# Summing the modulation over partitions: 32x32 transposes and small copies in place of products with ones

## The chip, the core and the metric

The kernel runs on one core of a Trainium2 chip. The core has five engines with a queue each that is worked in order: TensorE (PE, with its weight loads shown as PEld), VectorE (DVE), ScalarE (ACT), GpSimd (POOL) and SyncE (SP), which here issues nearly all transfers. The metric is the device time of one execution in microseconds (us); lower is better. A profile is one further execution, recorded by the hardware.

## The reference, cut to what matters

Two decoder layers of width 1024 over 512 tokens, each an attention (stick-breaking in layer 0, forgetting in layer 1) and a gated MLP of width 2816. Every layer is steered by a vector `mod` of 6 x 1024 numbers, which is made from the conditioning vector `c`:

```python
c_act = jax.nn.silu(c)
for i in range(DEPTH):
    mod = jnp.einsum('bd,dm->bm', c_act, w_mod[i]) + b_mod[i]
    sh_a, sc_a, gt_a, sh_f, sc_f, gt_f = jnp.split(mod, N_MOD, axis=-1)
    h = modulate(rmsnorm(x, g_mix_pre[i]), sh_a, sc_a)          # h * (1 + scale) + shift
    ...                                                         # qkv, attention, w_o
    x = x + gt_a[:, None, :] * rmsnorm(o, g_mix_post[i])
    h = modulate(rmsnorm(x, g_ffn_pre[i]), sh_f, sc_f)
    ...                                                         # gate, up, conv, silu, down
    x = x + gt_f[:, None, :] * rmsnorm(y, g_ffn_post[i])
```

All is float32. `mod` is a product of one row of 1024 numbers with a 1024 x 6144 matrix per layer. Its six parts of 1024 numbers (SH_A, SC_A, GT_A, SH_F, SC_F, GT_F) are needed in two shapes: the shifts and scales as columns (channel d*128+p on partition p, a tile of 128 x 8), the gates as rows that are the same on all 128 partitions (128 x 1024).

## The kernel before, in words

TensorE does every large product as three products of float32r halves (`mm3`, L320 to L322: high times high, low times high, high times low). Weights come as tiles of 128 x 1024 by SP (`raw`, L252, tile `wf`, three buffers), ScalarE writes the rounded half `wh` (L246), VectorE or GpSimd the rest `wl` (L247). `ws.need` loads two tiles ahead of the one that TensorE is about to use. In the MLP's first stage one iteration `f` of 22 has 24 products for `gate` and 24 for `up` (tile `pgu`, 128 x 512 each), then `conv_act` (tiles `cv`, `yh`, `yl`) on ScalarE and VectorE, which there also makes both `wl`.

The parts of `mod` are made in the background of other stages, by generators that are stepped at fixed places:

- `mod_part` makes GT_F of layer 0 and five parts of layer 1 during the MLP of layer 0, and GT_F of layer 1 during the MLP of layer 1. After every iteration `f` from 2 on, `bg.step(4)` takes four steps. Eight steps load one 512 KB tile `wm` each (L142) and add it, times a column of silu(c), into `acc` (128 x 1024, L146, VectorE; the first addition of a column part is L144). So each partition p of `acc` holds the sum over d of the terms of row d*128+p, and what is left is the sum over the 128 partitions. For that `acc` is split into `ah` and `al` (L149, L151), and a product with a 128 x 128 matrix of ones puts the sum on all partitions (L163, L164: two products for each half of 512 columns, tile `pm`). A gate is then multiplied by its norm's weights `gp` (L166). A shift or scale is on every partition in full, and the wanted column of 128 is its diagonal, taken eight times with a product by the identity and a sum (`diagonal`, L131).
- `mod_part_pe` makes GT_A, SC_F and SH_F of layer 0 during layer 0's attention, with the sum over rows on TensorE (L202), four row groups apart, each in its own 32 partitions. For a shift or scale ScalarE copies the result to `mf` (L209), four 128 x 128 transposes on TensorE (L220) turn it, and VectorE adds the four groups (L221).
- `begin` makes SH_A and SC_A of layer 0; the change does not touch it.

The order on PE and SP is the order of the program text; the other three engines are ordered by a scheduler when the program is built, except in `begin`. Tiles `wm`, `ah`, `al`, `gp`, `gb` share three buffers of 128 x 1024 (`t4`), and SP waits at a load until its buffer is free, with all later loads behind it.

Of the kernel before, what the change touches and what calls it, by code (L numbers as in the profile page):

```python
# [8 lines left out]
F32 = mybir.dt.float32  # L9
F32R = mybir.dt.float32r  # L10
BF16 = mybir.dt.bfloat16
AF = mybir.ActivationFunctionType
ALU = mybir.AluOpType
AX = mybir.AxisListType

P = 128
# [21 lines left out]
def trunk(ctx, tc, x, c, w_mod, b_mod, g_mix_pre, g_mix_post, w_qkv, w_o, w_fg, b_fg,  # L38
# [8 lines left out]
    def nm(s):  # L47
        serial[0] += 1
        return f"{s}_{serial[0]}"

    def bank(s="b"):
        return pp.tile([P, 512], F32, tag="bank", name=nm(s), bufs=8)
# [7 lines left out]
    def t4(s, dt=F32):  # L60
        return sb.tile([P, D], dt, tag="t4", name=nm(s), bufs=3)
# [4 lines left out]
    def junk(n=512):  # L66
        return sb.tile([P, n], BF16, tag=f"junk{n}", name=nm("junk"), bufs=1)
# [58 lines left out]

    made = {}

    def diagonal(dst, src):

        nc.vector.tensor_tensor_reduce(junk(P), src, idn, 1.0, 0.0, op0=ALU.mult, op1=ALU.add, accum_out=dst)  # L131

    def mod_part(l, comp):
        row = comp in (GT_A, GT_F)
# [5 lines left out]
        for d in range(ND):  # L140
# [4 lines left out]
            else:  # L145
                nc.vector.scalar_tensor_tensor(acc, w, csil[:, d : d + 1], acc, op0=ALU.mult, op1=ALU.add)  # L146
            yield
        ah = t4("ah", F32R)
        nc.scalar.copy(ah, acc)  # L149
        al = t4("al", F32R)  # L150
        nc.vector.tensor_tensor(al, acc, ah.bitcast(F32), op=ALU.subtract)  # L151
        if row:
            res = sb.tile([P, D], F32, tag="gt", name=nm("gt"), bufs=2)
            gp = t4("gp")
            g = (g_mix_post if comp == GT_A else g_ffn_post)[l]
            nc.sync.dma_start(gp, g.rearrange("(o n) -> o n", o=1).to_broadcast([P, D]))
        else:
            res = cst.tile([P, ND], F32, name=nm("mc"))
        yield
        for h in range(2):  # L160
            cs = slice(512 * h, 512 * h + 512)
            ps = bank("pm")
            nc.tensor.matmul(ps, ones, ah[:, cs], start=True, stop=False)  # L163
            nc.tensor.matmul(ps, ones, al[:, cs], start=False, stop=True)  # L164
            if row:
                nc.vector.tensor_tensor(res[:, cs], ps, gp[:, cs], op=ALU.mult)  # L166
            else:
                for j in range(4):
                    diagonal(res[:, 4 * h + j : 4 * h + j + 1], ps[:, j * P : (j + 1) * P])
            yield  # L170
        if not row:
            nc.vector.tensor_tensor(res, res, b_col(l, comp), op=ALU.add)
            if comp in (SC_A, SC_F):
# [3 lines left out]
    def mod_part_pe(l, comp):  # L177
# [7 lines left out]
        for h in range(2):  # L185
# [18 lines left out]
            if row:  # L204
                a = slot("mh"), slot("ml")
                split(*a, ps)
            else:
                f = slot("mf", F32)
                nc.scalar.copy(f, ps)  # L209
            yield  # L210
            ps = bank("pm")
            cs = slice(512 * h, 512 * h + 512)
            if row:
                for i in range(2):
                    nc.tensor.matmul(ps, ones, a[i], start=i == 0, stop=i == 1)
                nc.vector.tensor_tensor(res[:, cs], ps, gb[:, 512:], op=ALU.add)
                nc.vector.tensor_tensor(res[:, cs], res[:, cs], gb[:, :512], op=ALU.mult)
            else:
                for j in range(4):
                    nc.tensor.transpose(ps[:, j * P : (j + 1) * P], f[:, j * P : (j + 1) * P], idn)  # L220
                nc.vector.tensor_reduce(res[:, 4 * h : 4 * h + 4], ps.rearrange("p (j q k) -> p j q k", q=4, k=32)[:, :, :, 0], axis=AX.X, op=ALU.add)  # L221
        if not row:
            nc.vector.tensor_tensor(res, res, b_col(l, comp), op=ALU.add)
            if comp in (SC_A, SC_F):
# [3 lines left out]
    class Background:  # L228
        def __init__(self, parts, make=mod_part):
            self.gens = [make(*p) for p in parts]  # L230

        def step(self, n=1):
            while n and self.gens:
                try:
                    next(self.gens[0])
                    n -= 1
                except StopIteration:
                    self.gens.pop(0)

# [747 lines left out]
```

## Time and profile before

| what | value |
|---|---|
| median of 3 runs | 1270.32 us (1270.16 to 1272.4) |
| the profiled execution's own time | 1270.56 us |
| its span, first to last instruction | 1268.8 us |
| mean granted TensorE clock | 0.999 |
| busy: PE, PEld | 1245.5 us (98%), 1029.5 us (81%) |
| busy: DVE, ACT, POOL | 680.4 us (54%), 597.9 us (47%), 268.4 us (21%) |
| layer 0: attention about, then MLP from | 65 to 240 us, 290 us |
| moved by DMA | 169.71 MB, 134 GB/s over the span |

The span is 1.8 us shorter than the execution's time, which also has what lies around the first and last instruction. Shares are means over all stages. Rows of a timeline give the start, the length and, in brackets, how long the engine had stood idle and whose work ended that. Matmuls are pipelined, so that a row of 0.39 us may start 0.23 us after the row above it.

### The profile page before, as it was taken

The numbers are of one execution on the slowest core, as the hardware profiler recorded it, in microseconds if no ns is written. First come the engines' busy times: TensorE is split into PE (matmuls) and PEld (weight loads), VectorE is DVE, ScalarE is ACT, GpSimd is POOL, SyncE is SP. The second block draws the span as 40 slices with busy tenths as digits, with TensorE's granted clock in tenths as the row PEclk, the third lists the DMA queues.
The fourth block names the chain that finished last, engine by engine and source line by source line (L and its number), as shares of the span: only waits on it lengthen the run. The fifth ranks groups of instructions, "written<-read, shape, count | busy, mean of one in ns | idle before, by whom it ended". The sixth has DMA issues, their size and how long they took to land.

```text
span 1268.8 us, 16979 instructions
## 1 busy us (share of the span) xinstructions
PE 1245.5 (98%) x6380; PEld 1029.5 (81%) x6380; DVE 680.4 (54%) x1157; ACT 597.9 (47%) x1117; POOL 268.4 (21%) x302
## 2 busy tenths in 40 slices
PE   6999999999999999999999999999999999999997
PEld 5877878789887888888887888877988888888886
DVE  6655444366788886422263565564685444442233
ACT  7577656565333334311375655664743333332121
POOL 4764544610000000000215554352000000000000
PEclk9999999999999999999999999999999999999999
DMA  9746424325587875223504344243073333332231
GB/s 296 213 147 219 126 92 159 89 78 165 167 248 223 275 223 160 86 98 100 151 1 129 123 133 116 90 128 104 26 248 95 94 99 100 100 100 87 96 100 67
DMA packets 178358, 169.71 MB, mean 134 GB/s; under 512 B 6984, under 2 KB 151776, under 8 KB 178275
## 3 DMA queue, kind: packets, MB, share of 16 engines
q1 hardware_dynamic: 178098, 168.56, 43.4%
q8 instruction: 50, 0.82, 0.3%
q14 instruction: 34, 0.27, 0.1%
q10 hardware_dynamic: 176, 0.07, 0.0%
HBM read 166.44 MB, written 2.16 MB: 133 GB/s over the span
## 4 chain that ended last, share of the span: by engine, by line
PE 84%; DVE 5%; ACT 4%; DMA 4%; issue 1%; POOL 1%; SPq 0%; ACTq 0%; POOLq 0%; DVEq 0%
PE pgu L321 11%; PE pgu L322 11%; PE pgu L320 11%; PE pd L321 6%; PE pd L320 6%; PE pd L322 6%; PE pqk L320 4%; PE pqk L322 4%; PE pqk L321 4%; PE ps L442 3%; PE po L492 3%; PE pv L320 3%; PE pv L322 3%; PE pv L321 3%; PE pa L480 2%; DMA wf<-in_w_ffn_gate_dram 2%
## 5 line engine op out<-in xcount | busy, mean ns | idle before, releaser
L246 ACT CAST wh<-wf 128x1024 fp32r<-128x1024 f32 (+2 forms) x178 | 185.3, 1041 | 313.0 <-PE pd L322 134.6
L321 PE MATMUL pgu<-htl,wh 128*128 128x512 f32 (+1 forms) x736 | 276.4, 376 | 0.6 <-DVE htl L382 0.6
L320 PE MATMUL pgu<-hth,wh 128*128 128x512 f32 (+1 forms) x736 | 276.4, 376 | 0.0
L322 PE MATMUL pgu<-hth,wl 128*128 128x512 f32 (+1 forms) x736 | 276.1, 375 | 0.0
L247 DVE TENSOR_TENSOR wl<-wf,wh 128x1024 fp32r<-128x1024 f32 x122 | 149.3, 1224 | 216.2 <-ACT wh L246 214.0
L321 PEld LDWEIGHTS pgu<-htl,wh 128*128 128x128 f32 x736 | 138.5, 188 | 26.2 <-DVE htl L382 1.0
L320 PEld LDWEIGHTS pgu<-hth,wh 128*128 128x128 f32 x736 | 138.5, 188 | 25.1
L322 PEld LDWEIGHTS pgu<-hth,wl 128*128 128x128 f32 x736 | 138.5, 188 | 24.8
L247 POOL TENSOR_TENSOR wl<-wf,wh 128x1024 fp32r<-128x1024 f32 (+3 forms) x56 | 129.7, 2320 | 122.6 <-ACT wh L246 110.4
L333 POOL TENSOR_TENSOR r<-v,mhalf 128x1 f32<-128x1 f32 x32 | 17.6, 549 | 449.1 <-DVE v L329 449.1
L320 PE MATMUL pd<-wh,yh 128*128 128x512 f32 x288 | 112.0, 389 | 0.0
L321 PE MATMUL pd<-wl,yh 128*128 128x512 f32 x288 | 112.0, 389 | 0.0
L322 PE MATMUL pd<-wh,yl 128*128 128x512 f32 x288 | 112.0, 389 | 0.0
L320 PE MATMUL pqk<-hth,wh 128*128 128x512 f32 (+1 forms) x240 | 94.3, 393 | 0.0
L322 PE MATMUL pqk<-hth,wl 128*128 128x512 f32 (+1 forms) x240 | 92.2, 384 | 0.3 <-POOL wl L247 0.3
L321 PE MATMUL pqk<-htl,wh 128*128 128x512 f32 (+1 forms) x240 | 92.1, 384 | 0.0
L899 ACT ACTIVATE cv<-cv 128x512 f32<-128x512 f32 x44 | 27.8, 632 | 108.8 <-DVE cv L898 102.6
L146 DVE SCALAR_TENSOR_TENSOR acc<-wm,csil,acc 128x1024 f32<-128x1024 f32 x52 | 66.7, 1283 | 14.0 <-DMA wm<-in_w_mod_dram 13.1
L320 PE MATMUL pv<-wh,hth 128*128 128x256 f32 (+1 forms) x224 | 68.6, 306 | 0.9 <-ACT hth L685 0.9
L322 PE MATMUL pv<-wh,htl 128*128 128x256 f32 (+1 forms) x224 | 66.9, 299 | 0.0
L321 PE MATMUL pv<-wl,hth 128*128 128x256 f32 (+1 forms) x224 | 66.7, 298 | 0.0
L320 PEld LDWEIGHTS pd<-wh,yh 128*128 128x128 f32 x288 | 54.1, 188 | 11.3
(208 smaller groups left out, 2209.7 us busy)
## 6 DMA issues: line engine op xcount, KB each, us to landing
wm<-in_w_mod_dram SPq DMA_DIRECT2D x80, 512.0 KB, 5.8
wf<-in_w_ffn_gate_dram SPq DMA_DIRECT2D x44, 512.0 KB, 4.9
wf<-in_w_ffn_up_dram SPq DMA_DIRECT2D x44, 512.0 KB, 4.8
wf<-in_w_ffn_down_dram SPq DMA_DIRECT2D x44, 512.0 KB, 3.5
wf<-in_w_qkv_dram SPq DMA_DIRECT2D x41, 512.0 KB, 5.6
wm<-in_w_mod_dram SPq DMA_DIRECT2D x32, 256.0 KB, 5.4
wf<-in_w_o_dram SPq DMA_DIRECT2D x16, 512.0 KB, 3.5
cum<-cumd SPq DMA_DIRECT2D x16, 512.0 KB, 5.6
```

What stands on the lines that cost most here:

```text
L146: nc.vector.scalar_tensor_tensor(acc, w, csil[:, d : d + 1], acc, op0=ALU.mult, op1=ALU.add)
L246: nc.scalar.copy(hi, src)
L247: (engine or nc.vector).tensor_tensor(lo, src, hi.bitcast(F32), op=ALU.subtract)
L320: nc.tensor.matmul(ps, ah, bh, start=first, stop=False)
L321: nc.tensor.matmul(ps, ah, bl, start=False, stop=False)
L322: nc.tensor.matmul(ps, al, bh, start=False, stop=last)
L333: nc.gpsimd.tensor_tensor(r, v, mhalf, op=ALU.pow)
L442: nc.tensor.matmul(ps[:, :n], q[hd][:, qs], k[hd][i][:, :n], start=i == 0, stop=i == 1)
L480: nc.tensor.transpose(ps[:, c : c + P], probs[qb][:, kb * P : (kb + 1) * P], idn)
L492: nc.tensor.matmul(po[HD * hd : HD * hd + HD, kb * P :], vt[p // 4, kb][:, e : e + HD], at[hd][kb], start=kb == 0, stop=kb == NT - 1, tile ...
L899: nc.scalar.activation(a, a, AF.Silu)
```

## The change

`mod_part` no longer splits `acc` and multiplies by ones. VectorE turns every 32 x 32 block of `acc` (`tr`) and adds along the free dimension (`part`, 128 x 32): now the 32 partitions of each quarter are summed, and four partial sums are left in four groups of 32 partitions. GpSimd copies the four groups side by side onto partitions 0 to 31 (`quad`), VectorE adds them (`qsum`). A column part is then put on its partitions by four small copies on GpSimd. A gate is turned once more (`gtr`, 32 x 32), written to DRAM as a row of 1024 numbers (`gtd`), read back to all 128 partitions (`gb`), and multiplied by `gp`. In `mod_part_pe` the same is done for shifts and scales from PSUM, with the small copies on VectorE. A step may now yield True, which ends a `bg.step(4)` early, so that a gate's write, read and multiplication fall into separate iterations.

```diff
+    def quadrants(src, n, engine):
+
+        u = sb.tile([32, P], F32, tag="quad", name=nm("quad"), bufs=1)[:, : 4 * n]
+        s = sb.tile([32, 32], F32, tag="qsum", name=nm("qsum"), bufs=1)[:, :n]
+        for i in range(4):
+            engine.tensor_copy(u[:, i * n : (i + 1) * n], src[32 * i : 32 * i + 32])
+        nc.vector.tensor_reduce(s, u.rearrange("p (i b) -> p b i", i=4), axis=AX.X, op=ALU.add)
+        return s
+
+    def columns_of(res, s, engine):
+
+        for j in range(4):
+            engine.tensor_copy(res[32 * j : 32 * j + 32, :], s.rearrange("p (d j) -> p j d", j=4)[:, j, :])
...
-        ah = t4("ah", F32R)
-        nc.scalar.copy(ah, acc)
-        al = t4("al", F32R)
-        nc.vector.tensor_tensor(al, acc, ah.bitcast(F32), op=ALU.subtract)
+        turned, part = t4("tr"), sb.tile([P, 32], F32, tag="part", name=nm("part"), bufs=1)
+        nc.vector.transpose(turned, acc)
+        nc.vector.tensor_reduce(part, turned.rearrange("p (b c) -> p b c", c=32), axis=AX.X, op=ALU.add)
         if row:
-            res = sb.tile([P, D], F32, tag="gt", name=nm("gt"), bufs=2)
             gp = t4("gp")
...
+        yield
+        s = quadrants(part, 32, nc.gpsimd)
+        if row:
+            rows = sb.tile([32, 32], F32, tag="gtr", name=nm("gtr"), bufs=1)
+            nc.vector.transpose(rows, s)
+            yield True
+            line = dr.tile([1, D], F32, name=nm("gtd"))
+            nc.sync.dma_start(line.rearrange("o (b r) -> (o b) r", r=32), rows)
+            yield True
+            wide = t4("gb")
+            nc.sync.dma_start(wide, line.to_broadcast([P, D]))
+            yield True
+            res = sb.tile([P, D], F32, tag="gt", name=nm("gt"), bufs=2)
+            nc.vector.tensor_tensor(res, wide, gp, op=ALU.mult)
         else:
             res = cst.tile([P, ND], F32, name=nm("mc"))
+            columns_of(res, s, nc.gpsimd)
         yield
-        for h in range(2):
-            cs = slice(512 * h, 512 * h + 512)
-            ps = bank("pm")
-            nc.tensor.matmul(ps, ones, ah[:, cs], start=True, stop=False)
-            nc.tensor.matmul(ps, ones, al[:, cs], start=False, stop=True)
...
-                for j in range(4):
-                    diagonal(res[:, 4 * h + j : 4 * h + j + 1], ps[:, j * P : (j + 1) * P])
-            yield
...
                 f = slot("mf", F32)
-                nc.scalar.copy(f, ps)
+                nc.vector.transpose(f, ps)
+                columns_of(res[:, 4 * h : 4 * h + 4], quadrants(f[:, ::32], 16, nc.vector), nc.vector)
...
-                for j in range(4):
-                    nc.tensor.transpose(ps[:, j * P : (j + 1) * P], f[:, j * P : (j + 1) * P], idn)
-                nc.vector.tensor_reduce(res[:, 4 * h : 4 * h + 4], ps.rearrange("p (j q k) -> p j q k", q=4, k=32)[:, :, :, 0], axis=AX.X, op=ALU.add)
...
-                    next(self.gens[0])
-                    n -= 1
+                    n = 0 if next(self.gens[0]) else n - 1
```

How the instructions of VectorE stand where a column part ends in the MLP of layer 0. Before (the last of the eight diagonals of SC_A of layer 1, `junk` and its accumulator read; `mc` is the part's column tile, `pm` what the product with ones has summed):

```order
L131 ISA junk_3915,mc_3822<-pm_3906,zid 128x128
L131 ISA mc_3822 128x1
L146 SCALAR_TENSOR_TENSOR acc_3919<-wm_3998,csil,acc_3919 128x1024
L172 TENSOR_TENSOR mc_3822<-mc_3822,colA 128x8
L247 TENSOR_TENSOR wl_3961<-wf_3958,wh_3960 128x1024
L174 SCALAR_TENSOR_TENSOR mc_3822<-mc_3822,colA 128x8
L897 SCALAR_TENSOR_TENSOR cv_3988<-pgu_3926,colB_86,cv_3988 128x511
```

The same part with the change (lines have moved by 10: L257 is what was L247, L907 to L910 what was L897 to L900, L156 what was L146):

```order
L159 STREAM_TRANSPOSE tr_4060<-acc_3891 128x1024
L910 TENSOR_TENSOR cv_3963<-cv_3963,pgu_3902 128x512
L257 TENSOR_TENSOR wl_3990<-wf_3987,wh_3989 128x1024
L257 TENSOR_TENSOR yl_3970<-cv_3963,yh_3969 128x512
L160 TENSOR_REDUCE part_4061<-tr_4060 128x32
L154 TENSOR_SCALAR acc_4078<-wm_4079,csil 128x1024
L135 TENSOR_REDUCE qsum_4065<-quad_4064 32x32
L184 TENSOR_TENSOR mc_4071<-mc_4071,colA 128x8
L186 SCALAR_TENSOR_TENSOR mc_4071<-mc_4071,colA 128x8
L257 TENSOR_TENSOR wl_4020<-wf_4017,wh_4019 128x1024
```

Eight diagonals with their accumulator reads and the subtraction became a transpose, two sums and the same closing additions; the second sum and the first addition stand behind copies on GpSimd, and the next `wl` stands behind both.

On SP, the loads from the end of GT_F of layer 0 on. Before:

```order
L156 DMA gp_3639<-in_g_ffn_post_dram 128x1024
L142 DMA wm_3650<-in_w_mod_dram 128x1024
L252 DMA wf_3655<-in_w_ffn_gate_dram 128x8x128
L252 DMA wf_3685<-in_w_ffn_up_dram 128x8x128
L142 DMA wm_3725<-in_w_mod_dram 128x1024
```

With the change:

```order
L164 DMA gp_3658<-in_g_ffn_post_dram 128x1024
L262 DMA wf_3671<-in_w_ffn_gate_dram 128x8x128
L262 DMA wf_3701<-in_w_ffn_up_dram 128x8x128
L172 DMA gtd_3741<-gtr_3667 32x32
L262 DMA wf_3745<-in_w_ffn_gate_dram 128x8x128
L262 DMA wf_3775<-in_w_ffn_up_dram 128x8x128
L175 DMA gb_3815<-gtd_3741 128x1024
L262 DMA wf_3819<-in_w_ffn_gate_dram 128x8x128
L262 DMA wf_3849<-in_w_ffn_up_dram 128x8x128
L152 DMA wm_3892<-in_w_mod_dram 128x1024
```

The write and the read of the gate's row stand between weight loads, two iterations of `f` apart from the next part's first `wm`, which has moved three iterations later. On TensorE nothing has moved: 28 products with `ones` (four for each of seven parts) and 16 transposes of `mf` are gone, and the rows around them have closed up.

More of the change, by code (lines that the diff above doesn't have):

```diff
@@ L127, in trunk @@
     made = {}
-    def diagonal(dst, src):
-        nc.vector.tensor_tensor_reduce(junk(P), src, idn, 1.0, 0.0, op0=ALU.mult, op1=ALU.add, accum_out=dst)
+    def quadrants(src, n, engine):
[8 more added lines that the diff above has]
+            engine.tensor_copy(res[32 * j : 32 * j + 32, :], s.rearrange("p (d j) -> p j d", j=4)[:, j, :])
     def mod_part(l, comp):
@@ L156, in mod_part @@
             nc.sync.dma_start(gp, g.rearrange("(o n) -> o n", o=1).to_broadcast([P, D]))
+        yield
[12 more added lines that the diff above has]
+            nc.vector.tensor_tensor(res, wide, gp, op=ALU.mult)
         else:
             res = cst.tile([P, ND], F32, name=nm("mc"))
+            columns_of(res, s, nc.gpsimd)
         yield
-        for h in range(2):
-            cs = slice(512 * h, 512 * h + 512)
-            ps = bank("pm")
[L163 to L167, printed above, removed]
-                for j in range(4):
-                    diagonal(res[:, 4 * h + j : 4 * h + j + 1], ps[:, j * P : (j + 1) * P])
-            yield
         if not row:
@@ L208, in mod_part_pe @@
                 f = slot("mf", F32)
-                nc.scalar.copy(f, ps)
+                nc.vector.transpose(f, ps)
+                columns_of(res[:, 4 * h : 4 * h + 4], quadrants(f[:, ::32], 16, nc.vector), nc.vector)
             yield
+            if not row:
+                continue
             ps = bank("pm")
             cs = slice(512 * h, 512 * h + 512)
[L213 to L218, printed above, removed]
-                for j in range(4):
-                    nc.tensor.transpose(ps[:, j * P : (j + 1) * P], f[:, j * P : (j + 1) * P], idn)
-                nc.vector.tensor_reduce(res[:, 4 * h : 4 * h + 4], ps.rearrange("p (j q k) -> p j q k", q=4, k=32)[:, :, :, 0], axis=AX.X, op=ALU.add)
+            for i in range(2):
+                nc.tensor.matmul(ps, ones, a[i], start=i == 0, stop=i == 1)
+            nc.vector.tensor_tensor(res[:, cs], ps, gb[:, 512:], op=ALU.add)
+            nc.vector.tensor_tensor(res[:, cs], res[:, cs], gb[:, :512], op=ALU.mult)
         if not row:
```

## The prediction

> **What bounds the kernel now.** I read the page first (busy shares, slices, chain of waits), then TensorE's timeline around the products that go, then VectorE, GpSimd and the loads there. From the page:
>
> ```profile
> PE 1245.5 (98%) x6380; PEld 1029.5 (81%) x6380; DVE 680.4 (54%) x1157; ACT 597.9 (47%) x1117; POOL 268.4 (21%) x302
> PE   6999999999999999999999999999999999999997
> PE 84%; DVE 5%; ACT 4%; DMA 4%; issue 1%; POOL 1%; SPq 0%; ACTq 0%; POOLq 0%; DVEq 0%
> ```
>
> TensorE is busy in every slice after the first, and 84% of the chain that ended last runs on it. A busy row is no proof of pace, so here is the pace, from TensorE's timeline in the MLP of layer 0:
>
> ```profile
> 337.03 0.39 PE L163 MATMUL pm<-ah,ones 128*128 128x512 f32 x1
> ...
> 337.96 0.39 PE L320 MATMUL pgu<-hth,wh 128*128 128x512 f32 x1
> ...
> 359.73 0.39 PE L320 MATMUL pgu<-hth,wh 128*128 128x512 f32 x1
> ```
>
> Between the last two rows lie two iterations, 96 products, without a gap: 21.77/96 = 0.2268 us each, 10.89 us an iteration. The four products with ones take the same step, 0.93 us in all. What is taken off TensorE here comes off the end, as long as nothing else sets the pace.
>
> **What goes from TensorE.** The groups by tile, and the places where one of them cost something else than its step:
>
> ```profile
> L163 PE MATMUL pm<-ah,ones x14: 388/392/499, 337.0 to 956.6; 128*128 128x512 f32 x14
> L164 PE MATMUL pm<-al,ones x14: 393/396/497, 337.3 to 956.8; 128*128 128x512 f32 x14
> L220 PE MATMUL pm<-zid,mf x16: 270/272/273, 150.8 to 221.4; 128*128 128x128 f32 x16
> ```
>
> ```profile
> 150.55 0.39 PE L322 MATMUL pqk<-hth,wl 128*128 128x512 f32 x1
> 150.79 0.60 PE L220 MATMUL pm<-zid,mf 128*128 128x128 f32 x4
> ...
> 151.69 0.40 PE L322 MATMUL pqk<-hth,wl 128*128 128x512 f32 x1
> ...
> 223.96 0.51 PE L442 MATMUL ps<-kh,qa 128*128 128x512 f32 x1 [1.62 <-POOL kh L433]
> ...
> 393.07 0.39 PE L322 MATMUL pgu<-hth,wl 128*128 128x512 f32 x1
> 393.45 0.50 PE L163 MATMUL pm<-ah,ones 128*128 128x512 f32 x1
> 395.29 0.50 PE L164 MATMUL pm<-al,ones 128*128 128x512 f32 x1 [1.34 <-DVE al L151]
> 395.62 0.40 PE L320 MATMUL pgu<-hth,wh 128*128 128x512 f32 x1
> ```
>
> Of the 28 products 26 go at 0.93/4 = 0.2325 us: 6.05 us. The other two stood in TensorE's queue behind the late `al`: from 393.07 to 395.62 are 2.55 us, less one step 2.32 us. With the change no product waits for these sums, so that goes too. The transposes come in four groups: from 150.55 to 151.69 are 1.14 us where three products alone take 0.68, so 0.46 us a group. The last group, up to 221.4, stands ahead of the wait for `kh` at 223.96, which would only grow by it; I count three groups, 1.38 us. Sum: 6.05 + 2.32 + 1.38 = 9.75 us.
>
> **What comes to VectorE and GpSimd in the MLP of layer 0**, where six of the seven parts end. VectorE's timeline, a group of the diagonals, GpSimd's nearest rows, and a wait:
>
> ```profile
> 446.60 1.22 DVE L247 TENSOR_TENSOR wl<-wf,wh 128x1024 fp32r<-128x1024 f32 x1
> 447.73 2.60 DVE L146 SCALAR_TENSOR_TENSOR acc<-wm,csil,acc 128x1024 f32<-128x1024 f32 x2
> 450.25 1.22 DVE L247 TENSOR_TENSOR wl<-wf,wh 128x1024 fp32r<-128x1024 f32 x1
> 451.38 0.75 DVE L897 SCALAR_TENSOR_TENSOR cv<-pgu,colB,cv 128x511 f32<-128x511 f32 x1
> 452.05 1.22 DVE L151 TENSOR_TENSOR al<-acc,ah 128x1024 fp32r<-128x1024 f32 x1
> ```
>
> ```profile
> L131 DVE CUSTOM_DVE_ANT_0 junk<-pm,zid x32: 278/285/293, 372.0 to 475.6; 128x128 bf16<-128x128 f32 x32
> L131 DVE DVE_READ_ACCUMULATOR2_ANT mc<- x32: 81/84/86, 372.2 to 475.8; 128x1 f32 x32
> ```
>
> ```profile
> L450 POOL MEMSET bt<- 128x1 f32 x64 | 4.2, 99 | 0.1
> L82 POOL TENSOR_SCALAR_AFFINE_SELECT mask<-mask 128x128 f32<-128x128 f32 x1 | 0.3, 292 | 0.0
> L333 POOL TENSOR_TENSOR r<-v,mhalf 128x1 f32<-128x1 f32 x32 | 17.6, 549 | 449.1 <-DVE v L329 449.1
> ```
>
> ```profile
> DVE xs L392 <- POOL r L333: 11.3, 16, 1.0
> ```
>
> From start to start a `wl` takes 1.13 us, an addition into `acc` 1.26 (two from 447.73 to 450.25), a `cv` 0.67, and I take 0.67 for the two other operations of 512 elements. One iteration without background is 2 x 1.13 + 4 x 0.67 = 4.9 us of VectorE. A column part before: 8 x 1.26 + 1.13 for `al` + 8 x 0.37 for the diagonals with their reads (0.285 and 0.084) + 0.2 to close = 14.4 us over 11 steps, 2.75 iterations: 10.1 us an iteration, of 10.89 + 0.93/2.75 = 11.2. With the change: 10.1 for the additions; the transpose and the sum of 128 x 1024 elements, which this trace lacks, touch as much as a `wl`: 1.13 each, and 0.13 for the sum's wait for the transpose (1.26 less 1.13 above, since an addition waits for the one before it); 0.4 for the small sum and the closing. 12.9 us over 10 steps, 2.5 iterations: 5.2 + 4.9 = 10.1 us an iteration, of 10.89. Bounds for the transpose and the sum: half a `wl` to two of them, 2.4 each.
>
> The copies on GpSimd add two trips a column part, during which VectorE may stand: a copy of 32 x 32 lies between the 0.10 us of L450 and the 0.29 us of L82, nearer the first by its size: 0.13. The trip there and back costs the mean wait of 11.3/16 = 0.71 less `r` itself, 0.16. So 4 x 0.13 + 0.16 = 0.7 us a trip (0.56 to 1.33; with a slow start as of L333's 0.549 each, 2.4). The scheduler has put other work between for about half of them. 1.4 us uncovered would make 10.7 us an iteration, still under 10.89. So VectorE holds out, narrowly, and its cover is the lead of the weights. The tightest `wl` that I found, and the chain of waits in that stretch, in order of time:
>
> ```profile
> 356.49 1.23 DVE L247 TENSOR_TENSOR wl<-wf,wh 128x1024 fp32r<-128x1024 f32 x1 [1.85 <-ACT wh L246]
> ```
>
> ```profile
> 338.30 5.17 DMA wf<-in_w_ffn_gate_dram
> ...
> 349.53 3.73 DMA wm<-in_w_mod_dram
> ...
> 355.05 8.34 DMA wf<-in_w_ffn_gate_dram
> ...
> 394.10 1.14 DVE al L151
> ```
>
> That `wl` is done at 357.7; its iteration starts on TensorE at 359.73, so 2.0 us early. And from 338 to 395 the chain does not run over TensorE at all but over loads, additions and `wl`: SP issues `wm` only when a `t4` buffer is free, with the next `wf` behind it. This background pipeline is near its own limit, and the change asks for a part every 27.2 us instead of 30.8. In its favour: at 338 it started late, because the first `wm` of the next part waited for the `pm` products to free a buffer; with the change three weight pairs pass there before a `wm`, and no buffer waits for TensorE. I add 0.6 us of new waits on TensorE, between none and the 1.4 us of one part's two trips.
>
> [...]
>
> **The rest.** In layer 0's attention VectorE takes over four transposes from PSUM with eight small copies and a sum each: about 0.67 + 9 x 0.17 (by the 128x4 sum of L221, 0.174) = 2.2 us, four times:
>
> ```profile
> L221 DVE TENSOR_REDUCE mc<-pm x4: 174/175/175, 151.4 to 223.3; 128x4 f32<-128x16 f32 x4
> 212.51 0.59 ACT L209 COPY mf<-pm 128x512 f32<-128x512 f32 x1 [1.09 <-PE pm L202]
> 214.46 1.22 DVE L453 TENSOR_TENSOR_SCAN om<-ps,zid 128x512 f32<-128x512 f32 x1 [1.61 <-ACT ps L452]
> ```
>
> They fall into that idle time ahead of `om`, and ScalarE, freed of `mf`, delivers what `om` waits for 0.6 us sooner: nothing. Were that cover gone, one `om` would be 2 us late, and TensorE needs it only a head later. On SP the write of `gtd` waits for `gtr` and `gb` for the write, with `wf` behind. The order has `gtr` right behind a `yl` and the small sum; in the first gate's place that `yl` is
>
> ```profile
> 329.86 0.69 DVE L247 TENSOR_TENSOR yl<-cv,yh 128x512 fp32r<-128x512 f32 x1
> ```
>
> so `gtr` would come about 331, and the `wf` behind the write is first needed two iterations later, after 359; nothing. If `gtr` were 20 us late, that `wf` would be late next. The seventh part, in layer 1's MLP, has nothing beside it.
>
> Sum, on the profiled execution's 1270.56 us (0.24 above the median shown, inside its spread): 1270.56 - 9.75 + 0.6 = **1261.4 us**.
>
> **Rivals.**
> 1. *The background pipeline takes over in layer 0's MLP.* For: the chain from 338 to 395, and VectorE's waits for the `wm` loads, 13.1 us for 52 additions, 0.25 each:
>
> ```profile
> L146 DVE SCALAR_TENSOR_TENSOR acc<-wm,csil,acc 128x1024 f32<-128x1024 f32 x52 | 66.7, 1283 | 14.0 <-DMA wm<-in_w_mod_dram 13.1
> ```
>
> Against: leads mostly longer than the 2.0 us shown, and `ah` and `al` no longer take `t4` buffers. If both trips stay uncovered at 1.33 us: 12.9 + 2.7 = 15.6 us a part, 6.2 + 4.9 = 11.1 an iteration, 0.2 us too much; with half of the waits for the 3.2 loads of an iteration, 0.4 us, it is 0.6 us, over some ten iterations 6, less 2.0 of lead: 4 us on 1260.8, **1264.8**.
> 2. *The weights set the pace there, not TensorE.* Then six parts' products and the stall give nothing, and only layer 1's 0.93, the transposes' 1.38 and the 0.93 of the first gate, ahead of that stretch, are left, 3.2 us: **1267.3**. Against: no gap between 337.96 and 359.73. [...]
> 3. *Slower: VectorE becomes the bound.* Place: the same ten iterations. Price: transposes and sums at 2.4 us each and copies at 0.549: 10.1 + 4.8 + 0.4 + 4.8 = 20.1 us a part, 8.0 + 4.9 = 12.9 an iteration, 2.0 too much, 20 us less 2.0: 1260.8 + 18 = **1279**. It decides from 2.5 x (10.89 + 1.18 - 4.9) = 17.9 us a part on, where the loss eats 9.75 + 2.0. For: neither operation is in the trace. Against: VectorE's rows of 1024 elements above lie between 1.2 and 1.3 us, whatever the operation.
>
> That the products do not go is no rival: the order of TensorE's instructions shows them gone and no other moved.
>
> **Chances.** Forecast 0.66, rival 1 0.16, rival 2 0.07, rival 3 0.08, others 0.03. A measurement of this kernel tells about 0.2%, 2.5 us, from no change. Faster: the forecast, most of rival 1 and half of rival 2, 0.82. Within 0.2%: 0.10. Slower: 0.08. Range: 1259.2 (no new wait, the fourth group counted, and 1 us of the wait for `kh` gone) to 1267.5, which takes in rivals 1 and 2.
>
> **What would show it.** TensorE's step stays 0.2268 us with no `pm` product in the MLP; no row of TensorE there waits for `wl`. VectorE's transpose and sum near 1.2 us each, GpSimd's copies near 0.13 us, VectorE's wait for them under 1 us. The wait for `kh` near 2.1 us. Wrong, if TensorE waits for `wl` in the iterations after the first gate by more than 2 us in all, or if weight loads land late behind `gtd` or `gb`.

## The result and the profile after

The changed kernel takes 1261.2 us in the median of six runs (1259.97 to 1263.33), the kernel before 1270.44 us in the runs beside them (1270.01 to 1272.4): a ratio of 0.9926, with a 95% interval of 0.9916 to 0.9936. The forecast was 1261.4 us. The profiled execution is the longest of the six, 1263.33 us with a span of 1261.2. What lies outside the span is 2.13 to 2.21 us in these six runs and 1.73 to 1.91 in every run of the other kernels here, the kernel before included. Nothing on record says why. By spans the changed kernel, with a median of 1259.0 us, is therefore about 0.4 us further ahead in each comparison below than by times.

From the page of the changed kernel, the busy times and the chain that ended last:

```profile
PE 1238.9 (98%) x6336; PEld 1025.3 (81%) x6336; DVE 698.1 (55%) x1143; ACT 587.9 (47%) x1106; POOL 281.2 (22%) x346
PE 89%; DVE 4%; ACT 3%; issue 1%; POOL 1%; DMA 1%; ACTq 0%; POOLq 0%; DVEq 0%
```

TensorE has lost work, VectorE and GpSimd have gained some, and TensorE's part of the chain has risen from 84% to 89%, DMA's fallen from 4% to 1%: the stretch from 338 to 395 us, in which the chain ran over loads and additions, is gone from it.

Where the time went is read from the first or last product of each stage on TensorE (the MLP of layer 0 has its first one at 278.95 us, ahead of the round 290 in the table before the prediction). The kernel before (first `pgu` of layer 0's MLP, first `pd`, last `pqk` of layer 1's attention, last `pgu` of layer 1's MLP):

```profile
278.95 0.28 PE L320 MATMUL pgu<-hth,wh 128*128 128x256 f32 x1
529.51 0.39 PE L320 MATMUL pd<-wh,yh 128*128 128x512 f32 x1
...
839.39 0.40 PE L322 MATMUL pqk<-hth,wl 128*128 128x512 f32 x1
...
1141.80 0.39 PE L322 MATMUL pgu<-hth,wl 128*128 128x512 f32 x1
```

The changed kernel at the same places, with the wait for `kh` in the attention of layer 0 ahead of them and the one for a `wl` in layer 1's attention between them:

```profile
222.52 0.50 PE L452 MATMUL ps<-kh,qa 128*128 128x512 f32 x1 [2.09 <-POOL kh L443]
...
279.07 0.28 PE L330 MATMUL pgu<-hth,wh 128*128 128x256 f32 x1
522.13 0.39 PE L330 MATMUL pd<-wh,yh 128*128 128x512 f32 x1
...
689.11 0.50 PE L332 MATMUL pqk<-hth,wl 128*128 128x512 f32 x1 [1.10 <-POOL wl L257]
...
832.90 0.40 PE L332 MATMUL pqk<-hth,wl 128*128 128x512 f32 x1
1134.43 0.39 PE L332 MATMUL pgu<-hth,wl 128*128 128x512 f32 x1
```

The first stage of layer 0's MLP, from the first `pgu` to the first `pd`, went from 250.56 to 243.06 us, 7.50 less; no row of TensorE waits in it. The last stretch, from the last `pqk` to the last `pgu`, went from 302.41 to 301.53, 0.88 less. Attention gave nothing in this execution: TensorE arrived at the first `pgu` 0.12 us later than before, and in layer 1's attention the wait for a `wl` of GpSimd (0.34 us before) took 1.10, which is most of the 0.89 us by which the stretch from the first `pd` to the last `pqk` became longer (309.88 and 310.77). So the MLPs carry the gain, and the open question is attention.

What VectorE and GpSimd took on, as groups by tile of the changed kernel (shortest, median and longest in ns):

```profile
L159 DVE STREAM_TRANSPOSE tr<-acc x7: 1232/1237/1246, 325.9 to 937.2; 128x1024 f32<-128x1024 f32 x7
L160 DVE TENSOR_REDUCE part<-tr x7: 1204/1211/1221, 327.7 to 939.0; 128x32 f32<-128x1024 f32 x7
L134 POOL COPY quad<-part x28: 200/202/1132, 329.0 to 941.0; 32x32 f32<-32x32 f32 x28
L141 POOL COPY mc<-qsum x16: 183/185/188, 388.2 to 470.3; 32x8 f32<-32x8 f32 x16
```

and VectorE's waits for it (us in total, times, longest):

```profile
DVE qsum L135 <- POOL quad L134: 3.0, 5, 1.0
DVE mc L184 <- POOL mc L141: 2.5, 4, 1.0
DVE gt L178 <- DMA gb<-gtd: 1.3, 1, 1.3
```

Transpose and sum cost what a `wl` of 1024 elements cost on VectorE before, 1.22 us. VectorE's share in two stretches of the MLP of layer 0 (the third pair of numbers is VectorE's busy time and instructions, the number after the five pairs the granted clock):

```profile
364.00:386.00 22.00, 22.00 (x99) 18.22 (x98) 18.05 (x19) 7.85 (x10) 0.00 (x0) 1.00 0.72 235
408.00:430.00 22.00, 22.00 (x99) 18.22 (x98) 19.65 (x23) 8.10 (x11) 2.42 (x8) 1.00 0.79 261
```

At the height of the parts VectorE is busy for about 19.4 of 22 us (the mean of the last four such stretches before 496 us), 9.6 us in an iteration of 10.89.

### The profile page after: what moved, and what is told of

It reads as the page before. It is cut to its first block, busy times and chain, and to the rows that moved or that the text cites. A ratio compares the mean times of both kernels' runs of the same rounds, so it can differ in the third digit from the quotient of the medians.

```text
span 1261.2 us, 16897 instructions
## 1 busy us (share of the span) xinstructions
PE 1238.9 (98%) x6336; PEld 1025.3 (81%) x6336; DVE 698.1 (55%) x1143; ACT 587.9 (47%) x1106; POOL 281.2 (22%) x346
## 4 chain that ended last, share of the span: by engine, by line
PE 89%; DVE 4%; ACT 3%; issue 1%; POOL 1%; DMA 1%; ACTq 0%; POOLq 0%; DVEq 0%
PE pgu L331 13%; PE pgu L330 13%; PE pgu L332 13%; PE pd L330 6%; PE pd L332 6%; PE pd L331 6%; PE pqk L330 4%; PE pqk L332 4%; PE pqk L331 4%; PE ps L452 3%; PE po L502 3%; PE pv L330 3%; PE pv L331 3%; PE pv L332 3%; PE pa L490 3%
## 5 line engine op out<-in xcount | busy, mean ns | idle before, releaser
L257 DVE TENSOR_TENSOR wl<-wf,wh 128x1024 fp32r<-128x1024 f32 x122 | 149.3, 1224 | 210.5 <-ACT wh L256 208.2
L257 POOL TENSOR_TENSOR wl<-wf,wh 128x1024 fp32r<-128x1024 f32 (+3 forms) x56 | 130.0, 2325 | 116.6 <-ACT wh L256 110.6
L156 DVE SCALAR_TENSOR_TENSOR acc<-wm,csil,acc 128x1024 f32<-128x1024 f32 x52 | 66.6, 1280 | 14.4 <-DMA wm<-in_w_mod_dram 13.8
L332 PEld LDWEIGHTS pd<-wh,yl 128*128 128x128 f32 x288 | 54.1, 188 | 11.3
```

What stands on the lines that cost most here:

```text
L257: (engine or nc.vector).tensor_tensor(lo, src, hi.bitcast(F32), op=ALU.subtract)
L332: nc.tensor.matmul(ps, al, bh, start=False, stop=last)
```

## The experiments

The theory: TensorE is the bound, so what leaves it is the gain, stage by stage. The rivals: the gain comes from the relief of other engines or another pace of the parts; VectorE is at its limit already; the attention part does not gain, or costs.

### One half of the change at a time

`mlp_alone` keeps `mod_part` as changed and puts the old `mod_part_pe` back:

```diff
-                nc.vector.transpose(f, ps)
-                columns_of(res[:, 4 * h : 4 * h + 4], quadrants(f[:, ::32], 16, nc.vector), nc.vector)
+                nc.scalar.copy(f, ps)
...
+                for j in range(4):
+                    nc.tensor.transpose(ps[:, j * P : (j + 1) * P], f[:, j * P : (j + 1) * P], idn)
+                nc.vector.tensor_reduce(res[:, 4 * h : 4 * h + 4], ...)
```

> The changed kernel with mod_part_pe put back (columns of attention by 32 copies of the sums and TensorE transposes, as before), so that only mod_part, the part that runs beside the MLPs, differs from the kernel before. Theory (TensorE is full, so its removed work and its removed stall are the gain): 26 products at 0.2325 us and the 2.32 us stall behind al, 8.4 us in all, so 1262.0 us; the wait of ps for kh at 222 us is again 1.62 us as before. If the step from 1.62 to 2.09 us in that wait and the fall of the granted clock to 0.94 between 210 and 240 us took the attention's share back in the changed kernel, then this kernel is no slower than the changed kernel (1261 to 1262 us) and its runs lie closer together, with a clock of 1.00 between 210 and 240 us. Rival (the attention part does give its 1.4 us): 1262.6 to 1263, clearly behind the changed kernel.

Measured: 1262.41 us (1261.12 to 1263.71), ratio 0.9937 (0.9924 to 0.995), 8.4 us under its 1270.79. That is the theory's figure to the tenth, which is partly luck, since the interval of the ratio reaches from 6.4 to 9.7 us. Its first MLP stage takes 243.04 us, as in the changed kernel, and the wait for `kh` is 1.62 us again, with no fall of the clock behind it. The runs do not lie closer together, though, and the median is 1.2 us over the changed kernel's (1.6 by spans), near the 1.4 us of the rival; the intervals overlap, so that attention gives this much is likely and not shown.

`att_alone` is the reverse, the kernel before with the new `mod_part_pe`:

```diff
-                nc.scalar.copy(f, ps)
+                nc.vector.transpose(f, ps)
+                columns_of(res[:, 4 * h : 4 * h + 4], quadrants(f[:, ::32], 16, nc.vector), nc.vector)
```

> The kernel before with only mod_part_pe changed (transpose and copies on VectorE in place of ACT's copy and four TensorE transposes of each half). Theory of the prediction: three of the four groups of transposes are saved, 3 x 0.46 = 1.4 us, so 1269.1 us. Rival (the wait for kh at about 222 us only grows, and the granted clock falls behind it): 1270.4 to 1271.5 us, with the wait at 2.1 us and a clock under 1.00 between 210 and 240 us.

Measured: 1272.92 us (1268.74 to 1274.32), ratio 1.0013 (1.0004 to 1.0022): slower, outside both expectations. TensorE's timeline of `att_alone` in layer 0's MLP shows where:

```profile
395.11 0.51 PE L177 MATMUL pm<-ah,ones 128*128 128x512 f32 x1 [1.57 <-ACT ah L163]
396.96 0.71 PE L178 MATMUL pm<-al,ones 128*128 128x512 f32 x1 [1.34 <-DVE al L165]
397.46 0.63 PE L332 MATMUL pgu<-hth,wh 128*128 128x512 f32 x1
397.89 0.63 PE L333 MATMUL pgu<-htl,wh 128*128 128x512 f32 x1
398.31 0.63 PE L334 MATMUL pgu<-hth,wl 128*128 128x512 f32 x1
```

The product with `ah`, which did not wait before, now waits 1.57 us as well, and behind the double stop the products step at 0.43 us in place of 0.2268. The whole stage takes 253.66 us, 3.1 more than before, while the arrival at the first `pgu` (279.11 us) is 0.16 us later. So the new attention alone saved nothing in this execution, and a stop was longer in it that the other half of the change abolishes. The halves do not add up: 1272.92 and 1262.41 would make 1264.5 by addition, and together they are 1261.2. The order of VectorE's, ScalarE's and TensorE's instructions in the MLP is the same as in the kernel before, and the chain that ended last shows where the lateness comes in. The first weight load of the stretch that the prediction looked at, in `att_alone`:

```profile
338.38 7.29 DMA wf<-in_w_ffn_gate_dram
```

In the kernel before it was issued at 338.30 us and landed after 5.17; what the chain runs over behind it comes 1.65 to 2.2 us later in `att_alone`, up to the late `ah`. Why this load took longer is open, and so is whether the new attention brings it about: three of the eleven runs lie at 1268.74 to 1270.66 us.

### The products by themselves

`dummy` puts four products of ones with ones back into each part; they wait for nothing and nobody reads them:

```diff
+        for h in range(2):
+            ps = bank("pm")
+            for i in range(2):
+                nc.tensor.matmul(ps, ones, ones_row, start=i == 0, stop=i == 1)
+            yield
```

> The changed kernel with 28 products of ones with ones put back into mod_part, four to a part, at the old places; nobody reads their result, their operands are constants, and they wait for no al. Each part has two steps more again, as in the kernel before. Theory (the products were TensorE time and nothing hid them): 28 x 0.2325 = 6.5 us more than the changed kernel, 1267.7 us, and no wait for VectorE beside them; of the 2.32 us of stall nothing comes back. Rival (what helped was ACT's and VectorE's relief, or the slower or faster pace of the parts): within 1 us of the changed kernel, 1261 to 1262 us.

Measured: 1267.56 us (1266.58 to 1270.41), ratio 0.9979 (0.997 to 0.9988), 6.4 us over the changed kernel. Its rows on TensorE, the group and the two ends of the first MLP stage:

```profile
L187 PE MATMUL pm<-ones x28: 388/392/395, 368.5 to 986.7; 128*128 128x512 f32 x28
```

```profile
277.92 0.28 PE L336 MATMUL pgu<-hth,wh 128*128 128x256 f32 x1
526.54 0.39 PE L336 MATMUL pd<-wh,yh 128*128 128x512 f32 x1
```

The stage takes 248.62 us, 5.56 more than in the changed kernel for 24 products: 0.232 us each. The kernel before, with the same 24 products, takes 1.94 us longer still: that is the stall behind `al`, 2.32 us less the 0.47 of the two products that stood in it, 1.85. That leaves 0.09 us for the relief of ScalarE and VectorE and for the pace of the parts.

`gates_ones` gives only the three gates their products with ones back, so their way through DRAM is gone:

```diff
-            line = dr.tile([1, D], F32, name=nm("gtd"))
-            nc.sync.dma_start(line.rearrange("o (b r) -> (o b) r", r=32), rows)
...
+            for h in range(2):
+                cs = slice(512 * h, 512 * h + 512)
+                ps = bank("pm")
+                nc.tensor.matmul(ps, ones, ah[:, cs], start=True, stop=False)
+                nc.tensor.matmul(ps, ones, al[:, cs], start=False, stop=True)
+                nc.vector.tensor_tensor(res[:, cs], ps, gp[:, cs], op=ALU.mult)
+                yield
```

> The changed kernel with the three gates of mod_part summed by products with ones again, as before, and the four column parts as in the change. So the way through DRAM (write of gtd, read of gb) and the steps that end early are gone, and 12 products and the split into ah and al are back. Theory (the way through DRAM costs nothing, the products 0.2325 us each): 2.8 us more, 1264.0 us; the stall behind al at 394 us does not come back, since it stood in a column part. Rival (the round trip and the shorter steps delay weights, so that part of this is won back): 1262.5 us or less. Other rival (a gate's products stand behind a late al as well): 1266 us.

Measured: 1263.65 us (1263.24 to 1266.63), ratio 0.9951 (0.9938 to 0.9964): 2.45 us more (2.9 by spans), for 12 products that come to 2.8 us at 0.2325 each. The way through DRAM costs nothing that shows beside that.

### The wait for kh and the granted clock

In the changed kernel the stretch behind the wait for `kh` ran at half speed. The same window of the changed kernel,

```profile
223.50:227.00 3.50, 3.50 (x13) 2.95 (x13) 2.18 (x2) 2.98 (x6) 3.50 (x6) 0.51 0.38 136
```

and of `dummy`, which has the same wait (2.08 us):

```profile
223.50:227.00 3.50, 3.50 (x24) 3.17 (x23) 2.05 (x2) 3.23 (x7) 3.42 (x6) 1.00 0.40 145
```

13 products against 24 in 3.5 us. Six kernels here share this attention and its wait of 2.08 to 2.09 us with the changed one (`att_alone`, `dummy`, `gates_ones`, and `copies_vec`, `turn2`, `turn5` below). In the profiled executions of three of the seven the clock fell there, and they reach the first `pgu` at 279.07, 279.11 and 279.61 us; in four it did not, at 277.30 to 278.29, in the mean 1.5 us earlier. The seven also reach the row that waits for `kh` up to 1 us apart (222.34 to 223.33 us). From that row on to the first `pgu` the three take 56.5 to 56.6 us and the four 55.0, the same as the kernel before and `mlp_alone`: the fall costs 1.6 us. Two experiments take the stop away in different ways.

`wl_vec` moves the 2.38 us of GpSimd that stand ahead of `kh` to VectorE, one weight tile's remainder:

```diff
-            ws.add((l, "o", p), lambda fn=fn, l=l, p=p: fn(w_o[l, p * P : (p + 1) * P, :].unsqueeze(1), D, nc.gpsimd))
+            ws.add((l, "o", p), lambda fn=fn, l=l, p=p: fn(w_o[l, p * P : (p + 1) * P, :].unsqueeze(1), D, nc.vector if (l, p) == (0, 2) else nc.gpsimd))
```

> The changed kernel with the remainder wl of one weight tile of layer 0 (the third of w_o, the one GpSimd works on just ahead of kh at 219 us) on VectorE in place of GpSimd. Theory (the wait of 2.09 us for kh at 222 us comes from GpSimd's 2.38 us on that wl, and the granted clock falls behind it): the wait falls to 0.5 us or less, the clock between 210 and 240 us is 1.00 in the profile, and the time is 1258 to 1259.5 us with runs within 1 us of each other. Rival (another wait takes its place: kl, oh or om on VectorE come later behind the moved remainder, 1.1 to 1.3 us on VectorE): 1260.5 to 1262 us with a wait of PE for VectorE in that place.

Measured: 1259.7 us (1259.53 to 1260.15), ratio 0.9916 (0.9902 to 0.9931), the fastest kernel and the narrowest runs. TensorE's timeline of `wl_vec`:

```profile
221.91 0.50 PE L452 MATMUL ps<-kh,qa 128*128 128x512 f32 x1 [0.62 <-POOL kh L443]
...
276.92 0.28 PE L330 MATMUL pgu<-hth,wh 128*128 128x256 f32 x1
519.75 0.39 PE L330 MATMUL pd<-wh,yh 128*128 128x512 f32 x1
```

The wait is 0.62 us in place of 2.09 and the clock there 1.00, with no new wait behind VectorE. Wait and time lie a little over the theory's 0.5 and 1259.5 us. The medians of this kernel and the changed one lie 1.5 us apart (1.15 by spans), but their ratios' intervals overlap, so that it is faster is likely and not shown.

`fill` leaves the wait and puts eight unread products into it:

```diff
+        for _ in range(idle):
+            nc.tensor.matmul(ps, ones, ones_row, start=True, stop=True)
```

> The changed kernel with eight products of ones with ones, 8 x 0.23 = 1.8 us, placed on TensorE just ahead of the one product with kh at 222 us that waits 2.09 us; they write the score bank, which the real product then starts anew, and nobody reads them. The wait for kh is as long as before, but TensorE works through nearly all of it. Theory (after a stop of about 2 us the granted clock falls in some executions, and that is what spreads the changed kernel's runs from 1260.0 to 1263.3 us): the runs lie within 1 us of 1260, the granted clock between 210 and 240 us is 1.00, and the first product of the MLP starts at 277.9 us and not at 279.1. Rival (the spread has nothing to do with the stop): the same spread of 3 us and a median of 1261.2 us. If the added products only come later themselves (behind something the real product waits for), the time is 1.8 us longer, 1263 us.

Measured: 1261.12 us (1259.98 to 1261.34), ratio 0.9918 (0.9904 to 0.9931). TensorE's timeline of `fill`:

```profile
219.84 1.99 PE L453 MATMUL ps<-ones 128*128 128x512 f32 x8
222.12 0.50 PE L455 MATMUL ps<-kh,qa 128*128 128x512 f32 x1 [0.30 <-POOL kh L444]
```

The extra work costs nothing, the clock stays at 1.00 and the first `pgu` starts at 277.15 us. That fits the mechanism and does not prove it, since four of the seven executions without the fill kept the clock too. And three of the four runs lie at 1261.0 to 1261.3, not near 1260: the spread is narrower, 1.4 us in place of 3.4, and not gone.

This stop is not the only place where the clock can fall, and the record has a measure for the executions that were not profiled: the mean granted clock of every run. In the profiled executions a mean of 0.999 goes with no stretch at half clock between the first 20 and the last 10 us, and one of 0.998 or less with one or more. The changed kernel's six runs sort by it: 0.999 at 1259.97, 1260.01 and 1260.80 us, 0.998 at 1261.60 and 1262.28, 0.997 at 1263.33. So their spread goes with the clock. The three slower runs of `fill` have 0.997 or 0.998, so the clock fell in them at another place, or at this one in spite of the fill. The measure does not say that the longer wait for `kh` makes falls more frequent: of the 46 runs of the kernel before that stand beside the experiments 23 have 0.999, and of the 27 of the changed kernel, `dummy`, `gates_ones` and `copies_vec` 17.

`wl_vec2` goes on from `wl_vec` and moves two more remainders to VectorE, against the wait for `wl` in layer 1's attention:

```diff
-ws.add(key, lambda src=src, inner=inner: w_tile(src, inner, nc.gpsimd))
+ws.add(key, lambda src=src, inner=inner, e=nc.vector if key[:3] == (1, "qk", 1) else nc.gpsimd: w_tile(src, inner, e))
```

> The kernel with wl of the third w_o tile on VectorE (wl_vec), and besides the remainders of the two weight tiles of the second head pair of layer 1 (query and key) on VectorE in place of GpSimd, because TensorE waited 0.9 us for one of them at 686 us. Theory (any stop that is taken off TensorE is a gain of its length while another engine has room): 1258.8 us, with no wait of pqk for wl over 0.3 us. Rival (VectorE is late there with qa, kl and fx behind the moved remainders, or the keys come later): 1259.5 to 1261 us with a new wait of TensorE for VectorE.

Measured: 1260.61 us (1259.85 to 1261.2), ratio 0.9922 (0.9909 to 0.9935): nothing gained. The wait for `wl` is gone from its profile, without a new one behind VectorE, so neither expectation fits whole: the time is the rival's, the new wait is missing. What its profiled execution shows is another fall of the clock, a little ahead of that place, behind a stop of 1.44 us, which the kernel before (1.44) and the changed one (1.45) have too:

```profile
669.08 0.39 PE L332 MATMUL pqk<-hth,wl 128*128 128x512 f32 x1
670.91 0.50 PE L452 MATMUL ps<-kh,qa 128*128 128x512 f32 x1 [1.44 <-POOL kh L443]
...
671.80 0.40 PE L330 MATMUL pqk<-hth,wh 128*128 128x512 f32 x1
672.04 0.45 PE L331 MATMUL pqk<-htl,wh 128*128 128x512 f32 x1
672.28 0.63 PE L332 MATMUL pqk<-hth,wl 128*128 128x512 f32 x1
672.71 0.63 PE L330 MATMUL pqk<-hth,wh 128*128 128x512 f32 x1
```

All four runs have a mean clock of 0.998, as the profiled one has, so each of them had a fall; where, the mean cannot tell.

### How much room VectorE has

`copies_vec` puts the small copies of `mod_part` on VectorE:

```diff
-        s = quadrants(part, 32, nc.gpsimd)
+        s = quadrants(part, 32, nc.vector)
...
-            columns_of(res, s, nc.gpsimd)
+            columns_of(res, s, nc.vector)
```

> The changed kernel with the small copies of mod_part (quad, and mc of a column part) on VectorE in place of GpSimd. Theory (TensorE is the bound and VectorE has room): VectorE gets 8 copies of 0.13 to 0.16 us a column part, 1.2 us, so 10.1 us in place of 9.6 an iteration of 10.89, and loses the waits for GpSimd (3.0 and 2.5 us in all): no change, 1260 to 1262 us. Rival (VectorE is already near its limit there, and GpSimd's copies are what keeps it under): 1264 us or more, with TensorE waiting for wl.

Measured: 1261.06 us (1260.27 to 1262.89), ratio 0.9916 (0.9903 to 0.993): the same as the changed kernel. The group in `copies_vec`:

```profile
L134 DVE COPY quad<-part x28: 157/169/173, 331.8 to 942.9; 32x32 f32<-32x32 f32 x28
```

A copy is even shorter on VectorE (0.169 against 0.202 us), and which engine makes them does not matter.

`turn2` and `turn5` do the transpose two and five times more, `turn2_wl` and `turn3_wl` two and three times more on top of `wl_vec`:

```diff
-        nc.vector.transpose(turned, acc)
+        for _ in range(3):
+            nc.vector.transpose(turned, acc)
```

> The changed kernel with the transpose of acc done three times in place of once (same input, same output): 2 x 1.24 = 2.5 us more of VectorE in each of the seven parts, 1.0 us an iteration. VectorE was busy 19.4 of 22 us there, 9.6 us an iteration; with this 10.6 of 10.89. Theory of the prediction (the bound is TensorE until a part costs VectorE 17.9 us; this one costs 15.4): 1260.5 to 1262.5 us, no wait of TensorE for wl over 1 us. Rival 1 of the prediction (the background pipeline with its waits for loads is at its limit earlier): 1264 us or more.

> The changed kernel with the transpose of acc done six times: 5 x 1.24 = 6.2 us more of VectorE a part, 2.5 us an iteration, 12.1 us of 10.89. Theory of the prediction (past 17.9 us a part VectorE sets the pace; this part costs 19.1): 1.2 us too much in each of about 12.5 iterations, 15 us, less 2 to 5 us of lead: 1271 to 1275 us, with waits of TensorE for wl in the MLP of layer 0 that sum to 10 us or more. Rival (there is much more slack, since the scheduler can move the background past the weights and the parts may simply come later): under 1266 us.

> The wl_vec kernel with the transpose of acc done three times (15.4 us of VectorE a part). On the changed kernel this cost 3.6 us in the median, while its profiled execution showed no wait of TensorE behind it and the MLP of layer 0 as long as before (243.3 against 243.1 us), but a granted clock of 0.94 in two stretches of 30 us. Theory (the extra work itself costs nothing, what was seen is the clock behind the wait for kh, which wl_vec takes away): 1259.5 to 1260.5 us. Rival (VectorE's margin is already gone in most executions, in which weights come late in the MLP): 1262.5 us or more.

> The wl_vec kernel with the transpose of acc done four times: 16.6 us of VectorE a part, 11.1 us in the 10.89 us of an iteration by busy time. Theory of the prediction (limit at 17.9 us a part with the lead used up): 1259.7 to 1262 us. If the limit lies where busy time alone fills the iteration, at 10.89: 0.2 us in each of 12.5 iterations, 2.5 us, 1262 us. Rival (the limit lies lower, because VectorE also stands waiting for loads): 1266 us or more, with waits of pgu for wh or wl.

| kernel | VectorE's work a part, estimated (12.9 plus 1.237 per transpose) | median (range) | ratio (95%) | first MLP stage in the profile |
|---|---|---|---|---|
| `wl_vec` | 12.9 us | 1259.7 (1259.53 to 1260.15) | 0.9916 (0.9902 to 0.9931) | 242.83 us |
| `turn2_wl` | 15.4 | 1261.26 (1260.13 to 1264.43) | 0.9934 (0.9922 to 0.9946) | 247.39 |
| `turn3_wl` | 16.6 | 1266.43 (1265.18 to 1270.9) | 0.9974 (0.9965 to 0.9982) | 252.76 |
| `turn2` | 15.4 | 1264.85 (1263.25 to 1265.54) | 0.9946 (0.9934 to 0.9958) | 243.27 |
| `turn5` | 19.1 | 1286.2 (1284.28 to 1286.47) | 1.0113 (1.01 to 1.0127) | 265.72 |

Against the expectations, `turn2` has the time of the rival, `turn2_wl` lies between theory and rival, `turn3_wl` is the rival's with its waits, and `turn5` lies beyond the theory. The 17.9 us of the prediction is the point where the loss has eaten the gain; the expectations of `turn2`, `turn5` and `turn3_wl` use it wrongly as the point where the loss begins. That one follows from the prediction's numbers as 2.5 x (10.89 - 4.9) = 15.0 us, and the runs agree with it as far as their steps allow: at 15.4 us (`turn2_wl`, against the median of `wl_vec` at 12.9) three of five runs lose 0.4 to 1.6 us and two about 4 to 5, at 16.6 all lose 5 us or more. `turn3_wl` waits in the MLP three times over 1 us, on TensorE:

```profile
424.00 0.50 PE L333 MATMUL pgu<-hth,wl 128*128 128x512 f32 x1 [2.31 <-DVE wl L258]
...
458.59 0.50 PE L333 MATMUL pgu<-hth,wl 128*128 128x512 f32 x1 [1.65 <-DVE wl L258]
...
493.74 0.50 PE L331 MATMUL pgu<-hth,wh 128*128 128x512 f32 x1 [2.30 <-ACT wh L257]
```

In `turn5` the waits add up to 14.9 us, and the clock adds to that. Its waits, and the windows behind three of them, with the granted clock at 0.51 to 0.53:

```profile
PE pgu L331 <- ACT wh L257: 12.5, 3, 7.9
...
PE pgu L333 <- DVE wl L258: 2.4, 3, 1.4
```

```profile
436.00:443.00 7.00, 5.57 (x14) 4.26 (x14) 6.62 (x8) 2.20 (x3) 0.00 (x0) 0.51 0.69 241
...
477.00:480.50 3.50, 3.50 (x10) 2.72 (x9) 3.46 (x5) 0.62 (x1) 0.00 (x0) 0.51 1.09 356
...
504.00:511.00 7.00, 3.37 (x7) 2.27 (x8) 4.96 (x5) 2.09 (x2) 0.00 (x0) 0.53 1.01 335
```

That is why the loss, 25.0 us against the changed kernel, is greater than the expected 10 to 14: TensorE's stage grew by 22.7 us, of which 14.9 are waits, and about half of the 12.4 us of TensorE's busy time in these windows, 6.2, went to the slower clock. `turn2` is explained in part: its profiled execution lost nothing in the MLP, but its clock fell twice, from 20.7 to 24.1 us and from 676.1 to 679.5, the second time behind a stop of 1.45 us for `kh`, and none of its five runs has a mean clock over 0.998. What the four others lost beside that, up to 4.3 us over the changed kernel's median, is open; late weights as in `turn2_wl` are a candidate that no profile of `turn2` shows.

## Why the prediction was right, step by step

- **What goes from TensorE in the MLPs: right.** The terms were 22 products at 0.2325 us and 2.32 us of stall in layer 0, 7.44 us, and 0.93 us in layer 1. Measured were 7.50 and 0.88; `dummy` has the products at 0.232 us by themselves and the stall apart from them, `mlp_alone` both at 8.4 us.
- **The transposes, 1.38 us: about right where the clock holds, wrong where it does not.** The wait for `kh` grew from 1.62 to 2.09 us as foreseen. Where the clock held, TensorE reached the MLP 0.7 to 1.7 us earlier than before; where it fell, at 279.07 to 279.61 us and so 0.1 to 0.7 later. The step that failed is that the wait for `kh` costs only its length: behind the 2.09 us the clock fell in three of seven executions, at 1.6 us each. By that share the term is worth about 0.6 us and not 1.38, an estimate from seven executions. That the step from 1.62 to 2.09 us made the fall likelier rests on those three against none of two (the kernel before, `mlp_alone`), and the clocks of the other runs do not bear it out.
- **0.6 us of new waits: mis-sized in place.** The MLP of layer 0 has none. In layer 1's attention, which the prediction did not look at, the wait for a `wl` of GpSimd ranged from 0.2 to 1.1 us over the kernels here, with 0.34 before. The two errors nearly cancel, which is part of why the sum came out at 0.2 us from the median: that closeness is luck. Without the 0.6 the sum gives 1260.8 us, and the changed kernel's three runs at a clock of 0.999 lie at or below that, the three others above, so in place of new waits it was the clock that took the time.
- **VectorE and GpSimd.** Transpose and sum were taken at 1.13 us each and are 1.237 and 1.211. That VectorE's rows of 1024 elements take 1.2 to 1.3 us whatever the operation does not hold for the first addition (L144, now L154), 0.74 us. The copies were taken at 0.13 us; they are 0.20, and four of them take 1.33 to 1.86 us for `quad` in six of the seven parts, not 0.5, since one of the four stands behind VectorE (the longest took 1.13 us; below), and 0.93 in the seventh. VectorE's waits for them are under or about 1 us each, as the prediction asked, 5.5 us in all; spread over the four column parts that is near the 1.4 us a part it had left uncovered. VectorE's busy time came out at 9.6 us an iteration for 10.1 predicted.
- **The margin.** The runs agree with a loss that begins near 15.0 us a part, as the prediction's numbers have it. Between 16.6 us (6.7 over `wl_vec`) and 19.1 us (25.0 over the changed kernel) a straight line passes the gain of 9.2 us at 16.9 us: by this estimate the break point is 1 us lower than the 17.9 given. The clock is part of that, which fell behind one of the three late weights of `turn3_wl` and at all three places of late weights in `turn5`. That `turn2` comes out at Rival 1's figure, 1264.8 us, is no evidence for it, since part of that time is clock and `turn2_wl` has the same work at 1261.26; rival 3's mechanism is `turn5`. Rival 2 is excluded by `dummy`: 24 products in that stage cost their full price. The lower end of the range, 1259.2 us, is given 0.15 us too low: its terms make 1260.81 - 0.46 - 1.0 = 1259.35.
- **GpSimd's copies beside VectorE: GpSimd waits, VectorE does not.** VectorE in the changed kernel, at two places where four copies for `quad` start while a row of it runs (a `wl`, and the first addition of a column part), and then GpSimd's copies there, the four for `mc`, and the four for `quad` at 498 us; VectorE stands idle beside these last eight:

```profile
411.62 1.21 DVE L257 TENSOR_TENSOR wl<-wf,wh 128x1024 fp32r<-128x1024 f32 x1
...
441.29 0.74 DVE L154 TENSOR_SCALAR acc<-wm,csil 128x1024 f32<-128x1024 f32 x1
```

```profile
411.83 1.80 POOL L134 COPY quad<-part 32x32 f32<-32x32 f32 x4 [22.76 <-DVE part L160]
...
441.50 1.33 POOL L134 COPY quad<-part 32x32 f32<-32x32 f32 x4 [26.54 <-DVE part L160]
443.30 0.86 POOL L141 COPY mc<-qsum 32x8 f32<-32x8 f32 x4 [0.47 <-DVE qsum L135]
...
498.05 0.93 POOL L134 COPY quad<-part 32x32 f32<-32x32 f32 x4 [2.51 <-DVE part L160]
```

  Alone four copies for `quad` take 0.93 us. Behind the `wl`, which ends at 412.83, they take 0.87 more, behind L154, which ends at 442.03, 0.40 more: the first copy takes 1.07 and 0.60 us in place of 0.20, so that it ends 0.07 us after VectorE's row at both places, and the other three follow. The two rows of VectorE are no longer than others of their kind (1.21 us, where the 122 `wl` of L257 take 1.20 to 1.26, and 0.74, where the four of L154 take 0.74 to 0.75). What holds the copies back is not shown; GpSimd waits, VectorE does not, and what VectorE had to do meanwhile covers most of it (at 411 us it waited 0.17 us for that `quad`).

## What to carry to other kernels

A small sum over partitions that a saturated TensorE does with ones can go to engines with room, and the gain is then the removed products' step plus any stop that they stood in, here 0.232 us a product and about 1.9 us of stall; work out first how much room the other engine has per iteration, because past it the loss is steep: 25.0 us here at 19.1 us of VectorE a part. Count a stop of TensorE at more than its length: behind one of 2.1 us the clock fell in three of seven executions here, at 1.6 us each time. Before reading a difference of 1 or 2 us between kernels, compare the mean clocks of their runs. Halves of a change need not add up: here one half alone was slower in the median, in the one profiled execution by a stop that the other half removes.

## What was not expected of the hardware

After a stop the granted clock can be at 0.50 for one stretch of about 3.4 us, and then whole again: from 223.5 to 226.9 us in the changed kernel, from 397.1 to 400.5 in `att_alone`, from 672.2 to 675.7 in `wl_vec2`. In `turn5` the stretches that begin at 436.1 us and, within the stop of 7.9 us, at 504.4 us are twice as long, 6.8 us each. A product of 512 columns then steps at 0.43 us in place of 0.2268. Stops of 1.44 and 2.09 us were followed by it in some executions and not in others of the same length.
